# RWKV scan: the first batch of triangular inverses holds two items instead of five

## The chip, the cores and the metric

The kernel runs on one core of one Trainium2 chip. The metric is the device time of one execution in microseconds (us). A core has five engines that each work through their own list of instructions in order: TensorE (PE; its weight loads are shown as PEld), VectorE (DVE), ScalarE (ACT), GpSimd (POOL) and SyncE (SP), whose list here holds nearly all DMA issues. An engine waits at an instruction until what it needs has arrived, and everything behind it in the list waits too.

## The reference

Two layers work on 1024 latent and 256 context tokens, 1024 wide. The first mixes by neighbourhood attention and mLSTM, the second by a bidirectional RWKV-7 scan; each is followed by a squared-ReLU MLP. The change lies in the scan of the second layer. For each of 16 heads (64 wide) and both directions it computes

```
def step(s, inp):
    rt, wt, kt, vt, at, bt = inp
    sa = jnp.einsum('bhij,bhj->bhi', s, at)
    s = s * wt[:, :, None, :] + sa[..., None] * bt[:, :, None, :] + vt[..., None] * kt[:, :, None, :]
    y = jnp.einsum('bhij,bhj->bhi', s, rt) if with_out else None
    return s, y
...
state, ys = lax.scan(step, state, tuple(time_major(t) for t in (r, w, k, v, a, b)), reverse=reverse)
```

first over the context (which only gives the starting state), then over the latent tokens.

## The kernel before, in words

The token-by-token recurrence is done in chunks of 64 tokens. Within a chunk the dependence of a token on the earlier ones of the same chunk is a 64 x 64 triangular system, so each chunk and head needs the inverse of a unit triangular matrix; the state is then carried from chunk to chunk.

**Units, items, batches.** A unit is a pair of heads in one direction: 8 pairs x 2 directions = 16 units. Two units, the two directions of one head pair, run at a time. A unit has 1280 tokens = 20 chunks, cut into 5 items of 4 chunks; its first item (m = 0) is the context. In the list of 80 items the two units alternate: item 0 is the first of the forward unit, item 1 the first of the backward unit, item 2 the second of the forward unit, and so on; a new pair of units begins at items 10, 20, 30 and so on. Items are grouped, in this order, into batches of five: 16 batches.

**What is done for an item and a batch.**
- `item_a` (L1882): loads the item's rows (tiles kar, css), makes the decayed operands on ACT, POOL and DVE (E, EI, q, kd, AR, BK; BK by L1917 and L1918 on DVE), multiplies them on PE (G, L1931), and masks the products into G on DVE (L1938, two instructions an item). The two 32 x 32 diagonal blocks of each of its 8 chunk matrices are written to DRAM (ga, L1946). When the last item of a batch is written, the whole batch is read back, one small matrix to a partition (P, L1951): 16 partitions an item, 80 for five items.
- `batch_b` (L1954): inverts all 32 x 32 blocks of the batch at once on DVE, in 31 steps of two instructions (prd, L1970; R, L1971), 62 in all, each across all partitions of the batch. POOL first clears R (L1965), and the result goes to DRAM (rt, L1974). P and R exist once, so the next batch's R can be cleared only when rt has been read out of the old one.
- `item_c` (L1978): reads its inverses back (TT, L1989), transposes one block on DVE (T, L1992), and builds the off-diagonal 32 x 32 block by two sets of small matmuls on PE (Q, L1997, and T, L2002) with copies on ACT between them. From then on the item is solved.
- `unit_chain` (L2008): the state recurrence itself. Each chunk step takes, in turn, px from the state Z (L2040), a copy xs, px from TT (L2052), a copy UV, pz (L2062) and a new Z; the outputs py (L2075, L2077) go to rw_y. Before a step is written it draws on `item_c` until its item is solved.

**What sets the order.** `rwkv_scan` (L2159) puts all of these generators into a heap. Each has a start time in made-up units, a step and a rank; the heap writes out the next piece of whichever is due first. An item is worth T = 12 units: the chain of item e starts at 12 e, its `item_c` at 12 e - 11, `batch_b` for the batch that begins at item a starts at 12 a - 66 (-60 for the first), and `item_a` up to 134 units ahead. A piece that needs another drains it first. The framework then builds each engine's list from the program, and moves instructions a little by its own estimates, so the lists on the engines are not quite the heap's order. On the engines themselves nothing is reordered across a wait.

After the last item `half` frees the tiles of `item_a` and `batch_b` and loads the first three blocks of the output projection (in_w_o, L90) into their place; `wo_phase` (L2388) follows the scan and waits for all of it.

Of the kernel before, what the change touches and what calls it, by code (L numbers as in the profile page):

```python
# [28 lines left out]
def drain(g):  # L29
    for _ in g:  # L30
        pass
# [1803 lines left out]
T = 12  # L1835
# [7 lines left out]
EX = 0  # L1843
EZ = 2
RP = (1, 2, 3, 4)
BATCHES = ()


class Unit:
# [24 lines left out]
def item_load(kk, dr, it):  # L1874
    p, z, i = it.u.p, it.u.z, it.i
    it.kar, it.css = kk.tmx([128, 3, 256], "kar", bufs=KB), kk.tmx([128, 2, 256], "css", bufs=KB)
    n = 3 if i else 2
    kk.nc.sync.dma_start(it.css, dr["css"][z, p, i])
    kk.nc.sync.dma_start(it.kar[:, 0:n], dr["kar"][p, i][:, 0:n])
# [74 lines left out]
def batch_b(kk, b):  # L1954

    nc = kk.nc
    V = nc.vector
    for it in b.items:
        drain(it.a)
    n_ = 16 * b.n  # L1960
    N = slice(0, n_)
    P3 = b.P[N]
    R = kk.tmx([128, 1024], "R", bufs=1)[N]
    R3 = R.rearrange("q (s t) -> q s t", s=32)
    nc.gpsimd.memset(R, 0.0)  # L1965
    nc.gpsimd.memset(R[:, 0:1024:33], 1.0)
    for s in range(31):
        n, w = 31 - s, s + 1
        pr = kk.tmx([128, 256], "prd")[N, :n * w].rearrange("q (x t) -> q x t", t=n)
        V.tensor_tensor(pr, P3[:, s, s + 1:32].unsqueeze(1).to_broadcast([n_, w, n]), R3[:, 0:w, s].unsqueeze(2).to_broadcast([n_, w, n]), ALU.mult)  # L1970
        V.tensor_tensor(R3[:, 0:w, s + 1:32], R3[:, 0:w, s + 1:32], pr, ALU.add)  # L1971
        yield
    b.rt = kk.dram.tile([n_, 32, 32], F32, name="rt", tag="rt%d" % b.n, bufs=3)
    nc.sync.dma_start(b.rt, R3)  # L1974
    yield


def item_c(kk, it):  # L1978

    nc = kk.nc  # L1980
    b = it.batch
    drain(b.b)
    S0, S1 = slice(0, 32), slice(32, 64)
    t = it.TT = kk.tmb([128, 8, 64], "TT", bufs=TB)
    nc.gpsimd.memset(t, 0.0)  # L1985
    for d in range(2):
        B = slice(32 * d, 32 * d + 32)
        a = 8 * b.n * d + 8 * it.e
        nc.sync.dma_start(t[B, :, B], b.rt[a:a + 8].rearrange("q s t -> s q t"))  # L1989
    T1 = kk.tmb([64, 8, 32], "T1", bufs=3)  # L1990
    yield
    nc.vector.transpose(T1[S0], t[S0, :, S0])  # L1992
    yield
    G = it.GA
    ps = kk.bank("Q")
    for e in range(8):
        nc.tensor.matmul(ps[S1, 32 * e:32 * e + 32], G[S0, e // 2, e % 2, S1], T1[S0, e, :], start=True, stop=True, tile_position=(0, 32))  # L1997
    nc.scalar.activation(T1[S1].rearrange("s q t -> s (q t)"), ps[S1, :256], AF.Copy)
    yield
    ps = kk.bank("T")  # L2000
    for e in range(8):
        nc.tensor.matmul(ps[S0, 32 * e:32 * e + 32], T1[S1, e, :], t[S1, e, S1], start=True, stop=True, tile_position=(32, 0))  # L2002
    nc.scalar.activation(t[S0, :, S1], ps[S0, :256].rearrange("s (q t) -> s q t", t=32), AF.Copy)
    it.solved = True
    yield
# [146 lines left out]
def pair_out(kk, C, dr, p, chains):  # L2152
    for c in chains:
        drain(c)
    for a in range(2):
        yield from readout(kk, C, dr, p, dr["y"][p], a, kk.tmp, lambda w, o: kk.nc.sync.dma_start(dr["cat"][p][:, w], o))


def rwkv_scan(kk, C, dr, half):  # L2159

    nc = kk.nc
    fixed = lambda nm, s, n, shape: [[kk.tmb(shape, "%s%d%d" % (nm, z, i), bufs=1) for i in range(n)] for z in range(s)]
    kk.Z, kk.xs = fixed("Z", GROUP, 2, [128, 128]), fixed("xs", GROUP, 2, [128, 128])
    kk.zero = kk.tmb([128, 128], "zero", bufs=1)
    for t in sum(kk.xs + kk.Z, [kk.zero]):
        nc.gpsimd.memset(t, 0.0)
    units = [Unit(p, z) for p in range(8) for z in range(2)]
    items = []
    for g in range(0, 16, GROUP):
        us = units[g:g + GROUP]  # L2170
        for s, u in enumerate(us):
            u.slot = s
            u.items = [Item(u, m) for m in range(5)]
            for a, b in zip(u.items, u.items[1:]):
                b.prev = a
        items += [u.items[m] for m in range(5) for u in us]
    sizes = list(BATCHES)
    jobs = []
    a = 0
    while a < len(items):  # L2180
        n = min(sizes.pop(0) if sizes else 5, len(items) - a)
        b = Batch(kk, items[a:a + n])
        b.b = batch_b(kk, b)
        jobs.append((T * a - (66 if a else 60), 2, 0.9, b.b))
        a += n
    for e in range(KB - 1):
        item_load(kk, dr, items[e])
    for u in units:
        u.chain = unit_chain(kk, dr, u, dr["y"][u.p, u.z])
    from itertools import islice  # L2190
    for e, it in enumerate(items):
        it.a = item_a(kk, C, dr, it, items[e + KB - 1] if e + KB - 1 < len(items) else None)
        it.c = item_c(kk, it)
        jobs.append((T * (e - it.e) + AS * it.e - (134 if e > it.e else 126), 1, 3.0, it.a))
        jobs.append((T * e - 11, 3, 2.7, it.c))
        jobs.append((T * e + 0 + 0 * it.u.z, 0, GROUP * 1.0, islice(it.u.chain, 12)))
        if it.u.z == 1 and it.m == 4 and it.u.p < 7:
            p = it.u.p
            jobs.append((T * e + 44, 4, 1.9, pair_out(kk, C, dr, p, (units[2 * p].chain, units[2 * p + 1].chain))))

    def middle():
        for it in items:
            drain(it.a)
        for it in items:
            drain(it.batch.b)
            it.kar = it.css = it.batch.P = None
        half()
        yield
    jobs.append((T * 75 + 0, 5, 1, middle()))
    heap = [(t, o, k, step, g) for k, (t, o, step, g) in enumerate(jobs)]  # L2210
    heapq.heapify(heap)
    while heap:
        t, o, k, step, g = heapq.heappop(heap)
        try:
            next(g)
        except StopIteration:
            continue
        heapq.heappush(heap, (t + step, o, k, step, g))
    kk.Z = kk.xs = kk.zero = None
# [124 lines left out]
def layer1_mixer(kk, I, X, mixer):  # L2344
# [34 lines left out]
    with tc.tile_pool(name="SC", reuse_waits="tile", bufs=2) as kk.TB:  # L2379
        rwkv_scan(kk, C, dr, half)  # L2380
# [203 lines left out]
```

## Time and profile before

| | us |
|---|---|
| median of 3 runs | 4299.41 |
| lowest and highest run | 4292.06, 4300.91 |
| the profiled execution | 4303.33 |
| its span, first to last instruction | 4301.5 |

The busy shares of the span are PE 90%, PEld 73%, DVE 58%, POOL 50%, ACT 45%, over 72621 instructions. The scan is the stretch from about 2576 us (the first operands of item 0) to about 3490 us, 914 us in all. The first MLP and the context part lie before it, the output projection and the second MLP behind it.

How to read the rows: a row of the timeline has start, duration, engine, line of the kernel, operation, tile written and tiles read, shape, how many instructions were merged, and in brackets how long the engine stood idle before it and what ended that. A row of windows has the stretch, its length, the busy time of PE, PEld, DVE, ACT and POOL with instruction counts, the granted TensorE clock (1.00 is full speed), the DMA share and GB/s. A row of waits has the waiting engine and line, what it waited for, the sum, the number of times, and the longest.

### The profile page before, as it was taken

What the parts mean: (1) busy time and instruction counts of PE and PEld (TensorE: products, weight loads), DVE (VectorE), ACT (ScalarE), POOL (GpSimd) and SP (SyncE); (2) the same over time, 40 slices, a digit from 0 to 9 for tenths busy, and PEclk for the clock granted to TensorE, in tenths of its full rate; (3) what the DMA queues carried; (4) which work ended last, traced back from release to release, by engine and by line L of the source; (5) the groups of instructions that cost most, each with busy time, mean ns of one, the idle gap of its engine ahead of it and who ended that gap; (6) DMA issues with size and microseconds to landing.
All of it is one profiled execution on the core that took longest, in us unless ns stands there. A gap on an engine that the chain in (4) does not pass through costs nothing. (4 is left out here: it accounts for less than half of the span.)

```text
span 4301.5 us, 72621 instructions
## 1 busy us (share of the span) xinstructions
PE 3888.8 (90%) x26653; PEld 3135.2 (73%) x26653; DVE 2506.5 (58%) x4056; ACT 1934.7 (45%) x4657; POOL 2169.1 (50%) x2176
## 2 busy tenths in 40 slices
PE   6999998996998997997989995999999986998999
PEld 3899976685787775785757754878778774887877
DVE  5320266518667844547685427677778635777673
ACT  4132365615233433435655533666666653332433
POOL 4112010027886765666543336455545334987776
PEclk9999999997999998998979996999989998999999
DMA  4414235522447554562233454444444351445653
GB/s 169 125 63 139 90 129 155 175 82 95 137 159 252 171 167 158 198 203 66 99 114 113 142 197 122 109 131 127 132 127 135 96 173 45 159 159 204 212 172 103
DMA packets 494129, 602.47 MB, mean 140 GB/s; under 512 B 161628, under 2 KB 320892, under 8 KB 493772
## 3 DMA queue, kind: packets, MB, share of 16 engines
q1 hardware_dynamic: 491084, 588.39, 43.2%
q0 software_dynamic: 2688, 9.44, 0.6%
q8 instruction: 210, 3.44, 0.3%
q14 instruction: 147, 1.20, 0.1%
HBM read 429.63 MB, written 163.86 MB: 138 GB/s over the span
## 5 line engine op out<-in xcount | busy, mean ns | idle before, releaser
L95 POOL TENSOR_TENSOR wl<-raw,wh 128x1024 fp32r<-128x1024 f32 (+1 forms) x172 | 356.3, 2076 | 680.6 <-ACT wh L94 627.9
L1040 PE MATMUL w<-t,rh 128*128 128x512 f32 x1792 | 582.9, 402 | 42.0 <-DVE t L95 22.8
L95 POOL TENSOR_TENSOR rl<-raw,rh 128x512 fp32r<-128x512 f32 x320 | 495.4, 1559 | 115.7 <-ACT rh L94 107.7
L94 ACT ACTIVATE rh<-raw 128x512 fp32r<-128x512 f32 x320 | 201.2, 631 | 555.1 <-PE w L1040 218.1
L1040 PEld LDWEIGHTS w<-t,rh 128*128 128x128 f32 x1792 | 342.9, 192 | 143.1 <-DVE t L95 42.7
L1040 PE MATMUL w<-t,rl 128*128 128x512 f32 x896 | 357.2, 399 | 0.9 <-POOL rl L95 0.9
L402 PE MATMUL pt<-wh,h 128*128 128x256 f32 x1600 | 289.3, 284 | 0.0
L94 ACT ACTIVATE wh<-raw 128x1024 fp32r<-128x1024 f32 (+1 forms) x172 | 153.7, 894 | 267.0 <-DMA raw<-in_w 71.0
L402 PEld LDWEIGHTS pt<-wh,h 128*128 128x128 f32 x1600 | 250.2, 192 | 0.0
L1970 DVE TENSOR_TENSOR prd<-P,R 80x31 f32<-80x31 f32 (+15 forms) x496 | 219.7, 443 | 25.0 <-POOL TT L1985 9.1
L402 PE MATMUL pt<-wl,h 128*128 128x256 f32 x800 | 226.7, 283 | 0.0
L1971 DVE TENSOR_TENSOR R<-R,prd 80x31 f32<-80x31 f32 (+15 forms) x496 | 215.6, 435 | 9.6
L1492 POOL TENSOR_TENSOR ss<-h 128x512 f32<-128x512 f32 (+1 forms) x128 | 150.8, 1186 | 108.5 <-DVE xt L1495 106.9
L1040 PEld LDWEIGHTS w<-t,rl 128*128 128x128 f32 x896 | 171.8, 192 | 38.5 <-POOL rl L95 2.1
L1931 PE MATMUL G<-AR,BK 64*128 64x128 f32 x1280 | 174.9, 337 | 21.6 <-POOL AR L1920 10.2
L1938 DVE TENSOR_TENSOR G<-G,c_gmask 128x512 f32<-128x512 f32 (+1 forms) x160 | 98.8, 630 | 149.0 <-PE G L1931 149.0
L1931 PEld LDWEIGHTS G<-AR,BK 64*128 64x128 f32 x1280 | 121.1, 212 | 52.6 <-issue 16.2
L842 POOL TENSOR_TENSOR am<-am 128x1 f32<-128x1 f32 x64 | 16.6, 259 | 279.0 <-ACT ap L841 264.0
L2027 PE MATMUL px<-UV,G 128*64 128x64 f32 x1280 | 145.3, 239 | 12.8 <-DVE G L1938 8.9
L402 PEld LDWEIGHTS pt<-wl,h 128*128 128x128 f32 x800 | 153.8, 192 | 0.0
L1145 DVE SCALAR_TENSOR_TENSOR r<-r 128x512 f32<-128x512 f32 x128 | 138.7, 1085 | 4.1
L1495 DVE SCALAR_TENSOR_TENSOR xt<-ss,c_hmu,xt 128x512 f32<-128x512 f32 (+1 forms) x128 | 118.6, 945 | 35.1 <-ACT xt L1494 24.5
(779 smaller groups left out, 11443.8 us busy)
## 6 DMA issues: line engine op xcount, KB each, us to landing
raw<-in_w SPq DMA_DIRECT2D x132, 512.0 KB
araw<-in_ada_w SPq DMA_DIRECT2D x80, 512.0 KB
hd<-t SPq DMA_DIRECT2D x128, 256.0 KB
raw<-in_w SPq DMA_DIRECT2D x128, 256.0 KB
r<-hd SPq DMA_DIRECT2D x110, 256.0 KB
hd<-r SPq DMA_DIRECT2D x96, 256.0 KB
kar<-rw_kar SPq DMA_DIRECT2D x64, 384.0 KB
css<-rw_css SPq DMA_DIRECT2D x80, 256.0 KB
```

Of the source, the lines that this page charges most:

```text
L94: self.nc.scalar.activation(hi, raw, AF.Copy)
L95: (eng or self.nc.gpsimd).tensor_tensor(lo, raw, hi.bitcast(F32), ALU.subtract)
L402: mm(ps[:, :n], xx[:, sl], ww[:, k % 4, :], start=(k == 0 and p == 0), stop=(k == KC - 1 and p == 2))
L1040: kk.nc.tensor.matmul(o, ww, xx, start=(first and p == 0), stop=(last and p == 2), skip_group_check=True)
L1145: V.scalar_tensor_tensor(t, t, 0.0, t, ALU.max, ALU.mult)
L1492: nc.gpsimd.tensor_tensor(S, h[:, q - 1:q - 1 + w], h[:, q + 1:q + 1 + w], ALU.add)
L1495: nc.vector.scalar_tensor_tensor(t, S, C["hmu"][:, s, c:c + 1], t, ALU.mult, ALU.add)
L1931: nc.tensor.matmul(pg[h][:, 128 * j:128 * j + 128], BK[HH[h], j, :], AR[HH[h], j, :], start=True, stop=True)
L1938: V.tensor_tensor(G[:, :, h, 0:m], ps.rearrange("q (c t) -> q c t", t=128)[:, :, 0:m], mask[:, :, 0:m], ALU.mult)
L1970: V.tensor_tensor(pr, P3[:, s, s + 1:32].unsqueeze(1).to_broadcast([n_, w, n]), R3[:, 0:w, s].unsqueeze(2).to_broadcast([n_, w, n]), ALU.mult)
L1971: V.tensor_tensor(R3[:, 0:w, s + 1:32], R3[:, 0:w, s + 1:32], pr, ALU.add)
L2027: nc.tensor.matmul(px[LO, HH[h]], it.GA[:, j, h, :], it.UV[:, j, HH[h]], start=(h == 0), stop=(n == 0), tile_position=(0, 0), skip_group_c ...
```

## The change

The first batch is cut to two items, item 0 and item 1, one of each unit. All later batches still have five, so they begin at items 2, 7, 12 and so on, and three items are left for the last: 17 batches instead of 16. The first batch's start in the heap moves from -60 to -98; all others keep 66 units ahead of their first item.

```diff
 EX = 0
 EZ = 2
 RP = (1, 2, 3, 4)
-BATCHES = ()
+BATCHES = (2,)
...
         n = min(sizes.pop(0) if sizes else 5, len(items) - a)
         b = Batch(kk, items[a:a + n])
         b.b = batch_b(kk, b)
-        jobs.append((T * a - (66 if a else 60), 2, 0.9, b.b))
+        jobs.append((T * a - 66 if a else -98, 2, 0.9, b.b))
         a += n
```

So the change adds one batch: 62 DVE instructions, two clears of R on POOL, one write of rt and one pair of reads of P. And it shifts which items share a batch.

Three places show what moves. First DVE, at the start of the first inverse. Before (the masks of items 4 to 7 stand ahead of it, two instructions an item; `x4` are those of items 5 and 6):

```order
L1938 TENSOR_TENSOR G<-G,c_gmask 128x4x128 x2
L1917 SCALAR_TENSOR_TENSOR BK<-q,kar 128x4x64
L1918 TENSOR_TENSOR BK<-kd,EI 128x4x64
L1938 TENSOR_TENSOR G<-G,c_gmask 128x4x128 x4
L1917 SCALAR_TENSOR_TENSOR BK<-q,kar 128x4x64
L1918 TENSOR_TENSOR BK<-kd,EI 128x4x64
L1938 TENSOR_TENSOR G<-G,c_gmask 128x4x128 x2
L1970 TENSOR_TENSOR prd<-P,R 80x31
L1971 TENSOR_TENSOR R<-R,prd 80x31
```

After (`x4` are the masks of items 4 and 5):

```order
L1917 SCALAR_TENSOR_TENSOR BK<-q,kar 128x4x64
L1918 TENSOR_TENSOR BK<-kd,EI 128x4x64
L1938 TENSOR_TENSOR G<-G,c_gmask 128x4x128 x4
L1970 TENSOR_TENSOR prd<-P,R 32x31
L1971 TENSOR_TENSOR R<-R,prd 32x31
L1970 TENSOR_TENSOR prd<-P,R 32x60
L1971 TENSOR_TENSOR R<-R,prd 32x2x30
```

The first inverse now follows the masks of items 0 to 5, where it followed those of items 0 to 7. Its operands come from items 0 and 1 alone, yet the masks of four more items stand ahead of it in DVE's list. The masks and BK of the items up to 10 and 12 that stood ahead of it or in it still end up ahead of its last instruction.

Second DVE again, at the start of the second inverse. Before, it is that of items 5 to 9, and the transposes (L1992) of items 0 to 4 are woven into it, the first two of them here:

```order
L1971 TENSOR_TENSOR R<-R,prd 80x2x30
L1992 STREAM_TRANSPOSE T_23639<-TT 32x256
L1970 TENSOR_TENSOR prd<-P,R 80x87
L1971 TENSOR_TENSOR R<-R,prd 80x3x29
L1970 TENSOR_TENSOR prd<-P,R 80x112
L1971 TENSOR_TENSOR R<-R,prd 80x4x28
L1970 TENSOR_TENSOR prd<-P,R 80x135
L1992 STREAM_TRANSPOSE T_23751<-TT 32x256
L1971 TENSOR_TENSOR R<-R,prd 80x5x27
L1970 TENSOR_TENSOR prd<-P,R 80x156
L1971 TENSOR_TENSOR R<-R,prd 80x6x26
L1970 TENSOR_TENSOR prd<-P,R 80x175
```

After, it is that of items 2 to 6, and only the transposes of items 0 and 1 are in it:

```order
L1971 TENSOR_TENSOR R<-R,prd 32x31
L1970 TENSOR_TENSOR prd<-P,R 80x31
L1971 TENSOR_TENSOR R<-R,prd 80x31
L1970 TENSOR_TENSOR prd<-P,R 80x60
L1971 TENSOR_TENSOR R<-R,prd 80x2x30
L1992 STREAM_TRANSPOSE T_23737<-TT 32x256
L1970 TENSOR_TENSOR prd<-P,R 80x87
L1971 TENSOR_TENSOR R<-R,prd 80x3x29
L1970 TENSOR_TENSOR prd<-P,R 80x112
L1971 TENSOR_TENSOR R<-R,prd 80x4x28
L1970 TENSOR_TENSOR prd<-P,R 80x135
L1992 STREAM_TRANSPOSE T_23822<-TT 32x256
```

The second inverse follows the first with nothing between them, and the transpose of item 2 stands behind its end, four instructions into the third inverse.

Third PE, where item 2 is solved (T_23902 before and T_23935 after are item 2's transposed block; the Z and xs names are the two units' states and copies). Before:

```order
L1931 MATMUL G<-AR,BK 128x128 x4
L1936 MATMUL bkt<-ident,BK 128x128 x4
L2040 MATMUL px<-Z_22994,AR 64x128
L2040 MATMUL px<-Z_22996,AR 64x128
L1997 MATMUL Q<-T_23902,G 32x32 x8
L2027 MATMUL px<-UV,G 64x64 x3
L2052 MATMUL px<-xs_22998,TT 64x64 x2
L2052 MATMUL px<-xs_23000,TT 64x64 x2
```

After:

```order
L2040 MATMUL px<-Z_22994,AR 64x128
L2040 MATMUL px<-Z_22996,AR 64x128
L2052 MATMUL px<-xs_22998,TT 64x64 x2
L2052 MATMUL px<-xs_23000,TT 64x64 x2
L2062 MATMUL pz<-UV,BKt 64x64 x4
L1997 MATMUL Q<-T_23935,G 32x32 x8
L2027 MATMUL px<-UV,G 64x64 x4
L2002 MATMUL T<-TT,T_23935 32x32 x8
L2040 MATMUL px<-Z_22995,AR 64x128
L2040 MATMUL px<-Z_22993,AR 64x128
```

Q of item 2 has moved behind the rest of the chunk step that it stood in; up to there PE's list is the same in both, masks and products of items 0 to 12 included.

Beside these three, at the end of the scan: SP's list had the write of the last batch's rt, the two TT reads of its first item, and then two loads of in_w_o; now, for the last batch of three items, the two loads stand between rt and the first TT.

## Prediction

> **What bounds the kernel now.** I read the waits of PE over the scan first, since PE is the busiest engine of the page. Each row is the waiting engine and line, the releaser, total us, times, and the longest.
>
> ```profile
> PE Q L1997 <- DVE prd L1970: 29.1, 8, 25.2
> PE G L1931 <- POOL AR L1920: 10.2, 4, 5.8
> ...
> PE Q L1997 <- DVE T L1992: 8.2, 4, 3.2
> ```
>
> One wait stands out: 25.2 us before Q, the first matmul that needs an inverse. The other waits for inverses come to 29.1 - 25.2 + 8.2 = 12.1 us over the whole scan. The windows say the same (PE busy is the first figure after the length, the granted clock the third from the end):
>
> ```profile
> 2610.00:2656.00 46.00, 11.28 (x92) 9.32 (x92) 38.45 (x90) 10.95 (x30) 29.42 (x60) 0.50 0.52 143
> 2656.00:2676.00 20.00, 20.00 (x145) 15.82 (x143) 11.14 (x30) 6.62 (x23) 2.32 (x6) 0.51 0.16 39
> 2676.00:2696.00 20.00, 18.19 (x249) 15.07 (x249) 13.99 (x34) 12.71 (x48) 11.06 (x22) 1.00 0.31 88
> ...
> 2700.00:2800.00 100.00, 96.59 (x1191) 80.37 (x1190) 69.83 (x177) 64.48 (x227) 44.81 (x109) 0.91 0.44 116
> 2800.00:2900.00 100.00, 94.58 (x1229) 79.46 (x1227) 76.43 (x203) 65.48 (x230) 52.43 (x111) 0.95 0.46 121
> ```
>
> From 2610 to 2656 us DVE sets the pace (38.45 of 46 us) and PE is nearly idle; from 2656 us on PE is full, in order, with little slack. So a delay of the chain of steps that PE once has is hardly made up later, and only the fill at the start is open to this change. In it I read DVE's timeline. The first inverse (items 0 to 4) runs from 2609.59 to 2647.06, the second (items 5 to 9) from 2652.23 to 2697.68:
>
> ```profile
> 2587.10 0.75 DVE L1938 TENSOR_TENSOR G<-G,c_gmask 128x256 f32<-128x256 f32 x2
> ...
> 2601.99 1.28 DVE L1938 TENSOR_TENSOR G<-G,c_gmask 128x512 f32<-128x512 f32 x2
> ...
> 2608.39 1.29 DVE L1938 TENSOR_TENSOR G<-G,c_gmask 128x512 f32<-128x512 f32 x2 [1.74 <-PE G L1931]
> 2609.59 0.17 DVE L1970 TENSOR_TENSOR prd<-P,R 80x31 f32<-80x31 f32 x1
> ...
> 2646.85 0.21 DVE L1971 TENSOR_TENSOR R<-R,prd 80x31 f32<-80x31 f32 x1
> 2652.23 0.18 DVE L1970 TENSOR_TENSOR prd<-P,R 80x31 f32<-80x31 f32 x1 [5.17 <-POOL R L1966]
> ...
> 2661.64 0.42 DVE L1938 TENSOR_TENSOR G<-G,c_gmask 128x256 f32<-128x256 f32 x1 [2.44 <-PE G L1931]
> ...
> 2674.25 0.69 DVE L1938 TENSOR_TENSOR G<-G,c_gmask 128x512 f32<-128x512 f32 x1 [3.63 <-PE G L1931]
> 2674.86 0.41 DVE L1970 TENSOR_TENSOR prd<-P,R 80x256 f32<-80x256 f32 x1
> ...
> 2684.08 0.69 DVE L1938 TENSOR_TENSOR G<-G,c_gmask 128x512 f32<-128x512 f32 x1 [2.16 <-PE G L1931]
> ...
> 2694.66 0.69 DVE L1938 TENSOR_TENSOR G<-G,c_gmask 128x512 f32<-128x512 f32 x1 [3.24 <-PE G L1931]
> ...
> 2697.47 0.21 DVE L1971 TENSOR_TENSOR R<-R,prd 80x31 f32<-80x31 f32 x1
> ```
>
> The masks shown are those of items 1, 5, 7, 11, 12, 13 and 14. PE's side is the row of Q for items 0 to 3, then 5 and 7, with the step in which item 2 is first used (px at 2680.22):
>
> ```profile
> 2653.63 1.03 PE L1997 MATMUL Q<-T,G 32*32 32x32 f32 x16 [25.22 <-DVE prd L1970]
> 2655.13 1.06 PE L2002 MATMUL T<-TT,T 32*32 32x32 f32 x16 [0.46 <-ACT T L1998]
> ...
> 2663.60 1.06 PE L1997 MATMUL Q<-T,G 32*32 32x32 f32 x16
> ...
> 2675.95 0.69 PE L1997 MATMUL Q<-T,G 32*32 32x32 f32 x16
> ...
> 2680.22 0.43 PE L2040 MATMUL px<-Z,AR 128*64 128x128 f32 x2
> ...
> 2685.35 0.69 PE L1997 MATMUL Q<-T,G 32*32 32x32 f32 x16
> ...
> 2708.08 0.66 PE L1997 MATMUL Q<-T,G 32*32 32x32 f32 x16 [0.44 <-DVE prd L1970]
> ...
> 2728.92 0.69 PE L1997 MATMUL Q<-T,G 32*32 32x32 f32 x16
> ```
>
> An item is used up every 10 us or so. The second batch is needed at item 5 and comes 0.44 us late: it is just in time now. After the change the second batch is needed at item 2.
>
> **The change, step by step.**
>
> *A batch of two costs DVE as much as one of five.* The 62 instructions keep their length along a partition; only the partitions fall from 80 to 32. No inverse on 32 partitions is in the trace. On 128 partitions 256 elements took 0.42 us (2661.64), on 80 partitions 0.41 (2674.86), so I take no saving; the other bound, 32/80 of the time, would take 0.6 of the bare 27 us worked out below, 16 us, off the first inverse and leave item 2 on time.
>
> *The first inverse: 2.2 us earlier.* By the new list it begins behind the mask of item 5, which ended at 2603.27, 6.3 us before 2609.59. But the masks and BK of the two items that it overtakes fall into it instead: two masked items at about 1.29 (2608.39) and two BK pairs at about 0.75 (two instructions as long as those of 2587.10), 4.1 us. It ends at 2647.06 - 2.2 = 2644.9. Bounds: 0 to 6.3 us earlier.
>
> *The second inverse now stands between the first and item 2.* P and R exist once, so it starts 5.2 us later (2647.06 to 2652.23, the clear of R waiting for rt to land), at 2650.1. Its own length was 2697.68 - 2652.23 = 45.5 us. Out of it fall the two waits for the masks of items 13 and 14 (2.16 + 3.24), these four masks (4 x 0.69) and one BK pair (0.75), 8.9 us in all; the transposes that leave it lie before the wait of 3.63 us at 2674.25, which soaks them up, since PE brings that mask no sooner. 36.6 us are left, so it ends at 2686.7. Bounds: 33 us (that wait gone as well) and 40 us.
>
> *From there to item 2.* From the first inverse's end to Q took 2653.63 - 2647.06 = 6.6 us (rt out, TT in, transpose), so Q of item 2 runs at 2693.3, not 2675.95. Behind Q come T 1.5 us later (1.06 long) and then px, at 2695.9 instead of 2680.22: **15.7 us later**. PE stands from about 2677 until then; queued behind Q are both units' chains, all later G and, through them, the masks. Adding the bounds one way, 8 us; the other, 21.
>
> *The clock: +3 us.* The granted clock was 0.51 for the first 20 us after the long idle time, and 1.00 afterwards. At 0.51 Q of items 1 and 2 lay 12.3 us apart, at 1.00 those of 2 and 3 lay 9.4 apart: about 3 us an item. A new stop of some 16 us should bring the low clock back; for 4 us (at least) to 20 us (as then) this is 1 to 5 us, and I take 12 us, one item. The Trainium skill, TensorE: Matmul & The Clock Gate, Part 1, says that an idle window of about 3.4 us halves the clock and about 3.4 us of sustained work restores it. That the stop throttles, the trace bears out; that 3.4 us restore it, it does not here (20 us). By the page this term would be 1 us and the sum 2 us less.
>
> *The third batch (items 7 to 11): 0, bounds 0 and +5.* Its inverse starts at 2686.7 + 5.2 = 2691.9, takes 45.5 us again, and Q followed such an end by 2708.08 - 2697.68 = 10.4 us: 2747.8. Q of item 7 is due five items after 2693.3, at about 2747.8 with the slow clock (2728.92 + 15.7 + 3 = 2747.6). A tie, as now.
>
> *The added batch itself: 0.* About 27 us of DVE (62 instructions at the group means below, 0.443 and 0.435) lie under a PE that is full, as does its clear of R on POOL.
>
> ```profile
> L1970 DVE TENSOR_TENSOR prd<-P,R 80x31 f32<-80x31 f32 (+15 forms) x496 | 219.7, 443 | 25.0 <-POOL TT L1985 9.1 <-POOL R L1966 5.7 <-DMA P<-ga 1.4
> L1971 DVE TENSOR_TENSOR R<-R,prd 80x31 f32<-80x31 f32 (+15 forms) x496 | 215.6, 435 | 9.6
> ```
>
> *The last batch: +3 us.* Before, the last batch (items 75 to 79) wrote rt, read TT, and then SP issued two weight loads; after, the last batch is items 77 to 79 and SP's list has the two loads ahead of its first TT.
>
> ```profile
> 3435.00 0.41 SPq L1974 DMA_DIRECT2D rt<-R  x1
> ...
> 3438.17 0.82 SPq L1989 DMA_DIRECT2D TT<-rt  x2
> 3439.05 0.92 SPq L90 DMA_DIRECT2D raw<-in_w_o  x2
> ```
>
> ```profile
> 3440.51 0.66 PE L1997 MATMUL Q<-T,G 32*32 32x32 f32 x16 [1.00 <-DVE T L1992]
> ...
> 3442.74 1.06 ACT L94 ACTIVATE wh<-raw 128x1024 fp32r<-128x1024 f32 x1 [1.16 <-DMA raw<-in_w_o]
> ```
>
> The first load was waited for until 3442.74, 3.7 us after its issue, so a TT behind both comes about 4 us later; and the margin there is small, since Q of item 75 already waited 1.00 us for its transpose. I take 3 of the 4.
>
> Bounds 0 and 9 us (both loads and DVE's readout rows ahead of that transpose).
>
> Sum: 15.7 + 3 + 0 + 0 + 3 = 21.7 us on the profiled execution's 4303.33, so 4325.0. The median of the runs is 3.9 us lower, 4299.41, so **4321 us**. Its own range, with the terms' middle halves, is 4311 to 4331.
>
> **Rivals.**
>
> *Worse: every batch late.* If the third batch misses its tie by 5 us and the last pays 9 instead of 3, the sum is 32.7, 4332. For it: each later batch is already served at the edge (0.44 and 1.00 us). Chance 0.15.
>
> *The delay is absorbed.* The chain is late but the inverses on DVE are not, so the 12.1 us of later waits for them vanish, and the last batch costs nothing: 15.7 + 3 - 12.1 = 6.6, 4306. Against it: DVE's inverses hold masks that wait for PE (2.16, 3.24), so they slip with the chain. Chance 0.14; it decides where those waits are PE's only slack.
>
> *Nothing changes:* 4299. The first Q and the second inverse stay where they were, and item 2 is ready in time. This needs the second inverse to end 6.6 us before 2675.95, near 2669, in under 20 us. Chance 0.05.
>
> *Faster: the early batch pays.* If DVE reached the first inverse soon after the masks of item 1 (2587.85), at about 2594 with ga and P in between, and both inverses ran at the bare 27 us, they would end at 2594 + 27 + 5.2 + 27 = 2653.2, Q of item 2 could run at 2659.8 and px at 2662.4 instead of 2680.22: -18 us, 4282. It breaks even when the second inverse ends by 2671. The list of DVE speaks against the start (four more items' masks stand ahead) and 37.5 us for the first against the bare price. Chance 0.06.
>
> **How the numbers follow.** The forecast has 0.60. A measurement of this kernel can tell about 0.2%, 8.6 us, from no change. Faster takes 0.06 and a little noise, 0.07; same takes "nothing changes" and over half of "absorbed", 0.14; slower the rest, 0.79. The range of 8 in 10 runs from 4300, which takes in most of "absorbed", to 4336, a little over the "worse" case.
>
> **What would show it.** Right: PE's first Q still near 2651 to 2654; a new wait of 13 to 20 us at Q of item 2, with the clock at 0.50 in it; two inverses of DVE back to back, the second ending near 2687; the scan's end 18 to 26 us later; a Q wait of 3 us or more at item 77. Wrong: if Q of item 2 runs by 2684, or the wait is there but the scan ends less than 9 us later. The first inverse starting before 2600 would break the first step, a third batch waited for by over 3 us the fifth.

## The result

The changed kernel took 4345.72 us (median of 4 runs, 4339.26 to 4350.66), the kernel before 4300.16 us beside it (4 runs, 4292.06 to 4301.35). The ratio is 1.0118, with a 95% interval of 1.0097 to 1.014: about 46 us are lost. The forecast was 4321 us, range 4300 to 4336: the direction was right, the size was half, and the measurement lies above the range.

The waits of PE in the profiled execution after (span 4348.8 us; before 4301.5), in the same view as before:

```profile
PE Q L1997 <- DVE prd L1970: 39.8, 7, 17.7
PE Q L1997 <- DVE T L1992: 31.4, 11, 7.1
...
PE px L2027 <- DMA UV<-rw_v: 8.2, 2, 4.1
```

The long wait of the fill (25.2 us before) is now two of 16 to 18 us. That was expected. What was not: waits for the transposed block T come to 31.4 us where they were 8.2, and two waits of 4.1 us for the UV loads are new.

To see where in the scan the time goes, both scans are cut at the same work: from the first mask to the copy behind Q of item 2, from there to that of item 36, of item 76, and of item 79. The columns are the stretch, its length, the busy time of PE, PEld, DVE, ACT and POOL with their instructions, the granted clock, the DMA share and GB/s. Before:

```profile
2583.97:2676.68 92.71, 49.03 (x394) 39.49 (x395) 66.22 (x152) 28.38 (x85) 54.43 (x124) 0.58 0.47 125
2676.68:3034.28 357.60, 341.01 (x4329) 285.63 (x4330) 264.19 (x692) 233.60 (x816) 177.50 (x395) 0.94 0.46 122
3034.28:3448.57 414.29, 387.06 (x4981) 326.70 (x4982) 309.66 (x804) 265.19 (x928) 204.24 (x401) 0.92 0.45 123
3448.57:3473.57 25.00, 23.35 (x347) 19.64 (x346) 9.73 (x23) 19.20 (x65) 10.67 (x10) 1.00 0.52 150
```

And after:

```profile
2575.10:2682.37 107.27, 51.30 (x409) 41.44 (x410) 77.56 (x189) 31.02 (x93) 58.53 (x136) 0.58 0.43 119
2682.37:3034.45 352.08, 332.30 (x4312) 279.63 (x4312) 268.79 (x692) 231.81 (x807) 175.50 (x382) 0.94 0.45 120
3034.45:3489.28 454.83, 413.91 (x4981) 349.44 (x4982) 311.37 (x828) 270.26 (x927) 198.79 (x401) 0.84 0.41 110
3489.28:3523.45 34.17, 25.65 (x345) 21.66 (x344) 9.44 (x23) 20.37 (x65) 12.85 (x10) 0.85 0.48 140
```

The fill costs 14.6 us, the next 34 items give 5.5 back, the 40 items after that lose 40.5, and the last three lose 9.2. Sum 58.8 us; the spans differ by only 47.3, as this execution reached its first mask 8.9 us earlier and lost 2.6 less behind the scan. (A stretch is read from one execution of each kernel; over the kernels of this case the first mask lies anywhere from 2570 to 2594 us.) The third row says how 40.5 us are lost: PE executes the same 4981 matmuls, but is busy 26.9 us longer at a granted clock of 0.84 instead of 0.92, and idle 40.9 us instead of 27.2.

The fill itself, on DVE (first mask, then the first and last row of the first inverse, of the second, and the start of the third):

```profile
2575.10 0.74 DVE L1938 TENSOR_TENSOR G<-G,c_gmask 128x256 f32<-128x256 f32 x2
...
2593.31 0.47 DVE L1970 TENSOR_TENSOR prd<-P,R 32x31 f32<-32x31 f32 x1
...
2611.42 0.41 DVE L1970 TENSOR_TENSOR prd<-P,R 32x256 f32<-32x256 f32 x1
...
2633.80 0.20 DVE L1971 TENSOR_TENSOR R<-R,prd 32x31 f32<-32x31 f32 x1
2639.08 0.19 DVE L1970 TENSOR_TENSOR prd<-P,R 80x31 f32<-80x31 f32 x1 [5.08 <-DMA P<-ga]
...
2674.26 0.21 DVE L1971 TENSOR_TENSOR R<-R,prd 80x31 f32<-80x31 f32 x1
2679.90 0.19 DVE L1970 TENSOR_TENSOR prd<-P,R 80x31 f32<-80x31 f32 x1 [5.44 <-POOL R L1966]
```

And some rows of Q on PE, of items 0 and 2, and the waits for T in front of items 17, 48 and 77:

```profile
2640.49 1.03 PE L1997 MATMUL Q<-T,G 32*32 32x32 f32 x16 [17.67 <-DVE prd L1970]
...
2681.31 1.03 PE L1997 MATMUL Q<-T,G 32*32 32x32 f32 x16 [16.05 <-DVE prd L1970]
...
2834.08 1.03 PE L1997 MATMUL Q<-T,G 32*32 32x32 f32 x16 [1.46 <-DVE T L1992]
...
3185.45 1.03 PE L1997 MATMUL Q<-T,G 32*32 32x32 f32 x16 [4.19 <-DVE T L1992]
...
3506.14 1.03 PE L1997 MATMUL Q<-T,G 32*32 32x32 f32 x16 [7.11 <-DVE T L1992]
```

What stands around such a change of batch in the middle of the scan? At 3091 us a batch ends, and this is SP's queue after:

```profile
3091.60 0.32 SPq L1974 DMA_DIRECT2D rt<-R  x1
...
3095.06 0.28 SPq L1951 DMA_DIRECT2D P<-ga  x1
3099.50 0.34 SPq L2156 DMA_DIRECT2D rw_cat<-ro  x1
...
3100.41 0.39 SPq L1951 DMA_DIRECT2D P<-ga  x1
3100.89 1.77 SPq L2017 DMA_DIRECT2D UV<-rw_v  x2
3102.72 1.09 SPq L1989 DMA_DIRECT2D TT<-rt  x2
```

Between the two halves of P stands `rw_cat<-ro`, the write of the readout of a finished pair (`pair_out`). It waits until 3099.50 for the readout's last multiplication, which runs on POOL only at 3098.21, behind the clear of R for the new batch and one of UV:

```profile
3096.44 0.95 POOL L1965 MEMSET R<- 80x1024 f32 x1
...
3098.21 1.26 POOL L2147 TENSOR_TENSOR ro<-ro,gt 128x512 f32<-128x512 f32 x1
```

So the second half of P, UV and TT leave SP after 3100, and the next inverse starts at 3103.58:

```profile
3103.58 0.19 DVE L1970 TENSOR_TENSOR prd<-P,R 80x31 f32<-80x31 f32 x1 [6.50 <-DMA P<-ga]
```

Before, the readout's write stood ten or more rows of SP's list away from rt and P. The same place of the scan in the kernel before:

```profile
3065.70 0.33 SPq L1974 DMA_DIRECT2D rt<-R  x1
...
3067.98 1.42 SPq L1951 DMA_DIRECT2D P<-ga  x2
...
3089.94 0.34 SPq L2156 DMA_DIRECT2D rw_cat<-ro  x1
```

Batches that begin at items 2, 7, 12 ... bring the change of batch to the moment at which a pair's readout runs. That this is what costs is one theory; the experiments test it.

### The profile page after: what moved, and what is told of

The parts are those of the page before. It is cut to its first block, busy times and chain, and to the rows that moved or that the text cites. A ratio compares the mean times of both kernels' runs of the same rounds, so it can differ in the third digit from the quotient of the medians.

```text
span 4348.8 us, 72710 instructions
## 1 busy us (share of the span) xinstructions
PE 3906.2 (90%) x26653; PEld 3152.9 (73%) x26653; DVE 2504.5 (58%) x4118; ACT 1943.3 (45%) x4657; POOL 2161.8 (50%) x2178
## 5 line engine op out<-in xcount | busy, mean ns | idle before, releaser
L95 POOL TENSOR_TENSOR rl<-raw,rh 128x512 fp32r<-128x512 f32 x320 | 482.8, 1519 | 123.1 <-ACT rh L94 121.2
L1970 DVE TENSOR_TENSOR prd<-P,R 80x156 f32<-80x156 f32 (+22 forms) x527 | 216.9, 412 | 41.3 <-DMA P<-ga 19.3
L1971 DVE TENSOR_TENSOR R<-R,prd 80x156 f32<-80x156 f32 (+22 forms) x527 | 217.8, 413 | 10.5 <-DMA UV<-rw_v 0.3
```

Of the source, the lines that this page charges most:

```text
L95: (eng or self.nc.gpsimd).tensor_tensor(lo, raw, hi.bitcast(F32), ALU.subtract)
```

## The experiments

All ratios are against runs of the kernel before in the same comparison, with 95% intervals; the us are the ratio's difference from 1 times the median of before there (4291 to 4295). For the two runs with the readout or its write moved in the kernel before, the medians alone give 60 us lost and 16 gained where the ratios give 53 and 18; one of the expectations uses the figures of the medians.

**First, what of the change counts:** the fill (theory FILL), the seventeenth batch (COUNT) or the place at which batches begin (PLACE).

The due time alone:

```diff
-BATCHES = (2,)
+BATCHES = ()
```

> BATCHES is () again and only the first batch's due time is -98 instead of -60: sixteen batches of five, begun at items 0, 5, 10 ... as before. PE's list is that of before; on DVE the first inverse merely stands a few BK and mask rows earlier. Theory FILL (the loss comes from the first batches and what is waited for in the fill), theory PLACE (the loss comes from batches that begin at items 2, 7, 12 ... of the scan, whatever the first batch holds) and theory COUNT (the loss is the added seventeenth batch) all expect 0 +- 6 us here. Over +15 us would say that the due time alone does it, and all three would fall.

Measured 1.0006 (0.999 to 1.0022), +3 us. Starting the first batch early does nothing that can be told.

Two, three, then fives, so that the place is as before from item 5 on:

```diff
-BATCHES = (2,)
+BATCHES = (2, 3)
```

> First batches of two and of three, then fives: seventeen batches, the first begins as early as in the changed kernel, the fill again has two inverses ahead of item 2, but from item 5 on batches begin at 5, 10, 15 ... as before. FILL: loses as the changed kernel does, +30 to +50 us. COUNT: +30 to +50 us as well, one batch more. PLACE: the loss goes, -5 to +12 us, and no growth of the delay from item 37 on.

Measured 1.0048 (1.0023 to 1.0072), +21 us: between the theories. The stretches tell more: its fill took 107.98 us, 15.3 more than before; items 2 to 36 lost another 7.1 (a new wait of 11.09 us stands at item 5); items 36 to 76 only 2.1, and the last three took 25.02 us, as before. So the small batches cost what they cost in the fill, and the large loss behind item 36 is absent although there are seventeen batches. COUNT falls.

A batch of seven first, so that the later batches begin where the changed kernel's do, with sixteen batches:

```diff
-BATCHES = (2,)
+BATCHES = (7,)
```

> A first batch of seven (due -98), then fives: sixteen batches, as many as before, no second inverse ahead of item 2, but from item 7 on batches begin where the changed kernel's do (7, 12, 17 ...). FILL: the new wait at item 2 is gone; the first inverse waits for the masks of items 5 and 6, some 10 us later than before, so 0 to +12 us. COUNT: the same 0 to +12. PLACE: +35 to +60 us, growing in the second half of the scan as in the changed kernel.

Measured 1.011 (1.0086 to 1.0133), +47 us: the whole loss, with no small batch at the start and no added one. The stretch from item 36 to 76:

```profile
3030.55:3476.53 445.98, 403.08 (x4981) 340.22 (x4982) 311.04 (x828) 270.20 (x926) 200.62 (x401) 0.87 0.42 112
```

31.7 us longer than before, with the lower clock. FILL falls for the larger part, PLACE stands.

The kernel before with the place shifted at item 35 only:

```diff
-BATCHES = ()
+BATCHES = (5, 5, 5, 5, 5, 5, 5, 7)
```

> The kernel before up to item 34, then one batch of seven, then fives that begin at 42, 47 ... 77 and a last one of three: sixteen batches, the fill untouched, the place of the batches shifted by two in the second half alone. FILL: 0 +- 5. COUNT: 0 +- 5. PLACE: +25 to +50 us, lost from item 42 on with waits of PE for the transposed block or for prd at 42, 47, 52 ..., and with a lower granted clock after them; if only the last batch of three and the end of the scan cost, +5 to +12.

Measured 1.0074 (1.0054 to 1.0093), +32 us, as PLACE said, but not evenly: item 42 was solved 27 us late against the kernel before, item 71 only 12, and item 79 32. The long batch itself and the last batches cost here; between them the delay shrank. From item 42 on the readout's write stands within five rows of rt or P here too. From the item ahead of a batch to the latest of its first three, the delay rises by 5 to 7 us at items 47, 52, 57, 62 and 67, where in the changed kernel it rises by 7 to 13; here more than that is given back in between. So what a batch at this place costs is not fixed by the place alone, and by itself this run would not have shown PLACE.

**Second, why the place counts.** Theory READOUT: because `pair_out` then runs at the change of batch. Theory UNIT: because of where a batch begins against the first items of a pair. Only the readout is moved now, the batches stay. In the changed kernel:

```diff
-            jobs.append((T * e + 44, 4, 1.9, pair_out(...)))
+            jobs.append((T * e + 68, 4, 1.9, pair_out(...)))
```

> The changed kernel with pair_out (the readout of a finished pair) due at T * e + 68 instead of T * e + 44. In SP's list the readout's write rw_cat <- ro then stands 14 to 20 rows behind one batch's rt and ahead of the next, as in the kernel before; in the changed kernel it stands within 5 rows of rt and P<-ga, between the two halves of P or just ahead of the UV and TT loads. Theory READOUT (the loss of the second half is the readout meeting the change of batch): the delay of 50 us that grows from item 36 to item 79 goes, the fill's 9 to 15 us stay, so +8 to +20 us against the kernel before. Theory UNIT (what counts is where a batch begins against the first items of a pair, whose chunk steps are others): the loss stays, +40 to +55 us.

And in the kernel before:

```diff
-            jobs.append((T * e + 44, 4, 1.9, pair_out(...)))
+            jobs.append((T * e + 80, 4, 1.9, pair_out(...)))
```

> The kernel before, batches of five untouched, with pair_out due at T * e + 80 instead of T * e + 44: rw_cat <- ro now stands within 5 rows of rt and P<-ga, as it does in the changed kernel. READOUT: +20 to +45 us, lost at the first items of batches in the second half, with PE waiting for T, prd or UV there and the granted clock at 0.5 behind the waits. UNIT: 0 +- 6 us.

The first measured 1.007 (1.0045 to 1.0095), +30 us: less than the changed kernel, more than READOUT expected. Its third and fourth stretch:

```profile
3027.68:3455.66 427.98, 393.87 (x4981) 332.62 (x4982) 312.78 (x829) 266.23 (x927) 204.74 (x402) 0.91 0.44 116
3455.66:3489.78 34.12, 27.81 (x348) 24.25 (x347) 1.71 (x4) 21.04 (x67) 10.86 (x7) 0.80 0.36 104
```

Of the 40.5 us of the third stretch 13.7 are left; the 9 us of the last three items stay in full. The second measured 1.0124 (1.0084 to 1.0165), +53 us, more than either theory said. Its second and third stretch:

```profile
2667.48:3049.93 382.45, 362.11 (x4330) 302.15 (x4331) 265.11 (x669) 233.90 (x816) 178.36 (x391) 0.88 0.42 112
3049.93:3500.19 450.26, 409.99 (x4981) 344.18 (x4982) 311.40 (x828) 268.65 (x930) 205.15 (x404) 0.86 0.43 116
```

The kernel before, with its batches untouched, loses 36.0 us in the third stretch (and 24.9 in the second) when its readout is put where the changed kernel's is. UNIT, which said 0, falls. That a readout due three items later costs something of its own was not tried apart; in the changed kernel one due two items later made the kernel faster.

The counter-test leaves the readout of seven pairs out of both kernels:

```diff
-    for a in range(2):
-        yield from readout(kk, C, dr, p, ...)
+    for j in range(8):
+        kk.nc.gpsimd.dma_start(dr["cat"][p][:, 128 * j:128 * j + 128], kk.zero)
+    yield
```

> The changed kernel with the readout of the first seven pairs left out (loads, sums, reciprocal root, transposes; instead zeros are written to rw_cat from POOL): its time is read against the kernel before with the same left out. READOUT: the two differ by the fill and the last batch alone, +15 to +25 us, and the delay doesn't grow from item 36 to 76. If batches beginning at items 2 and 7 cost by themselves: +40 to +55 us.

> The kernel before with the readout of the first seven pairs left out in the same way: the base for the run of the changed kernel without it. Faster than the kernel before by what the readout now costs the scan, 10 to 40 us.

Against the whole kernel before they measured 0.9986 (0.9974 to 0.9997) and 0.9984 (0.9962 to 1.0007): without the readout the change costs 1 us, give or take 11, less even than expected. (Leaving it out also frees other work: in the stretch from item 36 to 76 of the changed kernel DVE is busy 262 us instead of 311 and POOL 154 instead of 199, so this pair of kernels alone could hide a loss that has another cause.) The stretches without readout, of the changed kernel:

```profile
2594.43:2714.39 119.96, 50.54 (x405) 40.67 (x406) 82.95 (x189) 30.88 (x93) 77.64 (x171) 0.60 0.45 123
2714.39:3049.58 335.19, 324.51 (x4282) 270.13 (x4282) 242.99 (x596) 227.05 (x802) 154.20 (x370) 0.96 0.44 112
3049.58:3437.44 387.86, 371.10 (x4917) 310.77 (x4918) 261.69 (x664) 255.66 (x908) 153.81 (x363) 0.94 0.40 99
3437.44:3465.92 28.48, 24.33 (x339) 20.58 (x338) 1.30 (x3) 19.85 (x65) 10.82 (x7) 0.88 0.45 133
```

and of the kernel before:

```profile
2586.68:2692.32 105.64, 49.79 (x389) 40.23 (x390) 70.47 (x150) 28.07 (x84) 70.66 (x160) 0.58 0.47 129
2692.32:3042.01 349.69, 338.32 (x4297) 281.69 (x4298) 242.15 (x595) 228.62 (x810) 161.77 (x381) 0.93 0.43 110
3042.01:3432.86 390.85, 377.15 (x4917) 315.90 (x4918) 257.50 (x643) 256.35 (x909) 159.71 (x364) 0.93 0.39 101
3432.86:3456.94 24.08, 22.05 (x339) 18.73 (x338) 1.30 (x3) 18.11 (x62) 6.38 (x6) 1.00 0.45 129
```

The fill loses 14.3 us here too, and the next 34 items give 14.5 back; the third stretch is 3.0 us shorter instead of 40.5 longer. That the readout would be worth 10 to 40 us to the kernel before was wrong: it hides there (-7 us, not told from none).

**Third, through which queue the readout acts.** Its write was taken out of SP's queue and issued from POOL, in three kernels: the changed one, the one before, and the one before with the readout at `T * e + 80`.

```diff
-  ... lambda w, o: kk.nc.sync.dma_start(dr["cat"][p][:, w], o))
+  ... lambda w, o: kk.nc.gpsimd.dma_start(dr["cat"][p][:, w], o))
```

> The changed kernel, the readout where it was, but its write rw_cat <- ro is issued from POOL, which also does the last multiplication on ro, so that it no longer stands in SP's list. READOUT by SP's queue (the write waits for the readout and holds back P, UV and TT behind it): most of the loss of the second half goes, +10 to +25 us against the kernel before. READOUT by DVE's list (its reductions and short rows stand ahead of the transposes and of prd): the loss stays, +35 to +50 us.

> The kernel before with rw_cat <- ro issued from POOL: what that alone does. By SP's queue: there the write stands apart from P, so little, -8 to +4 us. By DVE's list: 0 +- 4 us.

> The kernel before with pair_out at T * e + 80 (which alone cost 60 us) and with rw_cat <- ro issued from POOL (which alone gained 16 us). If the collision acts through SP's queue, -15 to +10 us against the kernel before. If it acts through DVE's list, +35 to +50 us. Both in equal parts: about +15 to +30 us.

Measured 1.0098 (1.007 to 1.0125), +42 us; 0.9958 (0.9943 to 0.9973), -18 us; 1.0048 (1.0032 to 1.0065), +21 us. The third stretch of the first:

```profile
3047.53:3467.49 419.96, 384.55 (x4981) 325.37 (x4982) 316.33 (x827) 268.07 (x927) 206.43 (x409) 0.92 0.45 118
```

That is 34.9 us shorter than in the changed kernel, but its other stretches grew, and the runs do not tell it from the changed kernel: by its expectation it speaks against SP's queue. The second missed its expectation, which gave at most 8 us of gain. So the base has moved: with the write on POOL in both, the change costs 42 + 18 = 60 us, no less than its 46, and of the change's own loss no part is shown to come from this write. The traces fit: SP stood 32.9 us in front of it before and 31.2 after.

For the readout at +80 the write gained 18 us where it stood apart from P, and 53 - 21 = 32 us where it stood beside it: about 14 us of that collision's 53 come from the write in SP's queue (uncertain by some 20 us, so it could be none), and 39 (uncertain by some 10) do not. The readout's loads stayed on SP in all of these runs. The remainder was not split further between them, DVE's rows of the readout, POOL's multiplication and PE's transposes.

The second of the three is faster than both kernels of this case, 4275.32 us against 4291.15 beside it.

**Last, the end of the scan.** The readout at +68 as above, and the job that drains the last inverse and issues the in_w_o loads two items later:

```diff
-    jobs.append((T * 75 + 0, 5, 1, middle()))
+    jobs.append((T * 77 + 0, 5, 1, middle()))
```

> The changed kernel with pair_out at T * e + 68 and, beside that, the weights' job at T * 77 instead of T * 75, so that the first TT of item 77 stands ahead of the in_w_o loads on SP and the last inverse is no longer drained in one piece. Theory READOUT with the last batch as a term of its own: the 9 us between items 76 and 79 go to 0 to 4, and against the kernel before +15 to +22 us are left (it was +28). If the weights' job is not what costs at the end, +26 to +32.

Measured 1.0023 (1.0009 to 1.0036), +10 us, below the 15 to 22 expected. The last three items:

```profile
3449.68:3477.01 27.33, 24.24 (x355) 19.94 (x354) 1.61 (x4) 20.64 (x67) 9.64 (x7) 1.00 0.46 135
```

27.33 us instead of 34.12 (25.00 before): with the readout moved, most of the last batch's loss is that job's place, as predicted in kind. With the readout and the job put back in step, 10 of the 46 us are left.

## Why the prediction was half right

- *A batch of two costs DVE as much as one of five:* right. 256 elements on 32 partitions took 0.41 us, on 80 partitions 0.41.
- *The first inverse 2.2 us earlier (bounds 0 and 6.3):* right within its bounds. Counted from the first mask, Q of item 0 ran at 2640.49 - 2575.10 = 65.4 us instead of 2653.63 - 2583.97 = 69.7, 4.3 us earlier. The wait in front of it fell to 17.67 us.
- *The second inverse between the first and item 2:* right. It started 5.08 us behind the first (5.2 predicted) and lasted from 2639.08 to 2674.47, 35.4 us (36.6 predicted).
- *Item 2 15.7 us later:* right within its bounds. At the px that the prediction names it was 13.0 us later (109.2 us from the first mask instead of 96.25), at the copy behind Q 14.6, with a new wait of 16.05 us at its Q and a clock of 0.52 in the 9.7 us behind it.
- *The clock behind it, +3:* at most that. Items 3 and 4 were 15.4 and 15.5 us late at that copy: 1 us more than item 2 there, 2.5 more than its px. Both terms together came to 15.5 instead of 18.7.
- *The third batch a tie:* right; at item 7 PE waited 0.24 us for it (0.44 at item 5 before), and the delay there was 14.2 us.
- *The added batch hidden, 0:* right; seven instead of two, with sixteen batches, loses the same 47 us, and two-three with seventeen does not lose it.
- *The last batch +3 (bounds 0 and 9):* mis-sized. It measured 9.2, the upper bound, with a Q wait of 7.11 us at item 77 (3 or more predicted) and 2.3 us more of PE's busy time at a clock of 0.85 instead of 1.00. Beside the two loads, rt left SP 7.2 us after the inverse's end (3485.40 to 3492.63, behind a UV load), where it took 0.8 before; the price of 3 us held neither that nor the clock.

With these terms alone the sum would be about 25 us. **The step that failed is the first reading: "only the fill at the start is open to this change".** It followed from PE being full there, and it left out that the change moves every later inverse by two items against everything that is not counted in batches. The readout is such a thing: it comes once in ten items, its write had stood clear of the change of batch on SP, and afterwards stood within five rows of it. In the traces the stretch from item 36 to 76 loses 40.5 us; with the readout moved back 13.7 of them are left, without the readout none. The runs show it from both sides: moving the readout alone costs the kernel before 53 us, moving it back gains the changed kernel 46 - 30 = 16 us (uncertain by some 14; 36 together with the job at the end of the scan), and without the readout the change costs nothing that can be told. How much of the 46 the readout's place costs by itself stays open: some 16 by the one, all of it by the other. Through which engine it costs stays open too.

The same step failed in the other direction as well. That "a delay of the chain of steps that PE once has is hardly made up later" held in part for the changed kernel, where 5.5 of 14.6 us came back by item 36. But with the readout moved 11.4 of 14.4 us came back, and without it all of 14.3. Without it PE's busy time from item 2 to 36 fell from 338.3 to 324.5 us, at a clock of 0.96 instead of 0.93, while its idle time stayed near 11 us: what came back is nearly all clock. What seems to give it back is in the waits: before, PE waited for masks where a new pair begins,

```profile
PE px L2027 <- DVE G L1938: 8.9, 5, 2.8
```

and after the change 0.5 us of those 8.9 are left; without the readout they go from 6.0 to none. In the trace these masks now fall between two inverses instead of into one. That this accounts for all of what came back was not tried.

The rival "every batch late" named the right kind of loss and gave it 11 us (5 for the third batch, 6 for the last). It missed that one wait is followed by others. Such a wait of the changed kernel, of 1.46 us (the row at 2834.08 above), with the 8 us up to it, the 6.6 us behind it and 8 more:

```profile
2826.00:2834.00 8.00, 6.15 (x70) 4.85 (x67) 4.79 (x11) 5.96 (x21) 4.41 (x9) 0.99 0.51 90
2834.00:2840.60 6.60, 6.52 (x64) 5.76 (x64) 6.22 (x18) 1.87 (x6) 2.67 (x5) 0.50 0.53 156
2841.00:2849.00 8.00, 7.56 (x116) 6.46 (x115) 5.80 (x18) 5.87 (x20) 3.59 (x6) 1.00 0.52 129
```

6.6 us at half the clock are 3.3 us of work lost, more than twice the wait. A slower PE also brings the masks later. In front of the wait of 4.19 us at 3185.45, DVE stood 7.24 us for a mask, and behind it the readout's rows and the inverse's steps had to go ahead of the transpose that PE wanted:

```profile
3176.91 0.69 DVE L1938 TENSOR_TENSOR G<-G,c_gmask 128x512 f32<-128x512 f32 x1 [7.24 <-PE G L1931]
...
3178.67 0.68 DVE L2121 TENSOR_TENSOR y<-y,y 128x512 f32<-128x512 f32 x1
...
3183.78 0.67 DVE L2132 TENSOR_REDUCE rds<-y 128x8 f32<-128x512 f32 x1
...
3184.88 0.43 DVE L1992 STREAM_TRANSPOSE T<-TT 32x256 f32<-32x256 f32 x1
```

This chain, from a short wait to a slow PE to a late mask to the next late batch, is read from the trace and was not tried by itself.

Why does the loss of the changed kernel show only behind item 36, while its readouts start at 2787 us, at item 13? The delays answer it in part. Counted as above, the delay rises by 4 to 7 us at each of items 17, 22, 27 and 32, and by 7 to 13 at each batch from 37 to 67. Up to item 36 this is offset by 5 us given back at each of items 13, 23 and 33, where the waits for masks are gone; behind it the rises outweigh what comes back. With the readout at +68 the rises up to item 47 are 1 to 4 us. Why the later ones are larger stays open.

## What to carry to other kernels

Where work of two periods shares in-order queues (here batches of five items and a readout every ten), a change of the first item shifts one against the other for the whole run: before costing the place that was edited, look in the order of each queue at what the moved work now stands next to, SP's queue included. A DMA that waits for a late producer belongs in a queue in which nothing urgent stands behind it; issuing one such write from the engine that makes its data gained the kernel before 18 us. And a wait of PE is priced with the clock behind it, not by its own length.

## What the hardware showed beside that

- A wait of 1.46 us, with 0.4 us more of idle time in the 8 us up to its end, was followed by 6.6 us at half the clock. So was every PE wait of 1.4 us or more in the scans of both profiled executions, before and after, by a clock of 0.50 within 4 us, while of the shorter ones some were (0.83 us at 3253.22 after) and some not (1.03 us at 3033.59 before). The Trainium skill, TensorE: Matmul & The Clock Gate, Part 1, gives one idle window of about 3.4 us for the throttle and about 3.4 us of sustained work for its release. The trace disagrees with both in this kernel: shorter waits throttle, and the slow stretch behind one took 6.6 us here and 20 us at 3101 to 3121 (clock 0.51), though PE was busy for 16.6 of those 20.

```profile
3101.00:3121.00 20.00, 16.61 (x134) 13.59 (x134) 15.64 (x36) 6.59 (x22) 10.29 (x18) 0.51 0.56 150
```

- Moving 14 writes of 0.34 us issue time each from SP to POOL gained the kernel before 18 us (12 to 24). The Trainium skill, DMA: Bandwidth & Descriptors, section "Issuing engines are not separate DMA queues", says that issuing from several engines saves only the sequencer's time to initiate them. By that it would be 14 x 0.34 = 4.8 us at most, an estimate; the measurement is larger. In the trace before, SP stood 32.9 us in all in front of this write, with the DMAs behind it in its list held back; that this makes up the difference is argued, not shown.
